# Moving the split of constant tables, the low parts of weights and the softmax scaling between engines in layer 0's mixer

## The chip, the cores and the metric

The kernel runs on one core of a Trainium2 chip. The metric is the device time of one execution in microseconds (us); the time of a version is the median of several executions. The core's engines are TensorE (PE; its weight loads are shown as PEld), VectorE (DVE), ScalarE (ACT), GpSimd (POOL) and SyncE (SP). Each works through a queue of its own in a fixed order, and waits on semaphores where it needs another's result. In this kernel SP issues all data transfers (DMAs).

## The reference

One step of a two-layer backbone on 128 context and 512 latent tokens, width 1024, in float32. Each layer is half an FFN, a token mixer and half an FFN. Layer 0's mixer, which the change touches, is windowed attention and a Hyena long convolution side by side; layer 1's is a gated DeltaNet. Cut to the mixer of layer 0:

```python
def sink_softmax(logits, sink):
    s = jnp.broadcast_to(sink.astype(jnp.float32).reshape(1, KVH_A, G_A, 1, 1), logits.shape[:-1] + (1,))
    return jax.nn.softmax(jnp.concatenate([s, logits], axis=-1), axis=-1)[..., 1:]
...
def hyena_mixer(u3, conv_w, conv_b, w1, b1, f1, w2, b2, f2, w3, bias):
    length = u3.shape[1]
    u3 = depthwise_conv(u3, conv_w) + conv_b
    x1, x2, v = jnp.split(u3, 3, axis=-1)
    kf = jnp.fft.rfft(hyena_filter(length, w1, b1, f1, w2, b2, f2, w3), n=2 * length, axis=0)
    z = v.astype(jnp.float32)
    for o, gate in enumerate((x1, x2)):
        y = jnp.fft.irfft(jnp.fft.rfft(z, n=2 * length, axis=1) * kf[None, :, o], n=2 * length, axis=1)[:, :length]
        z = gate.astype(jnp.float32) * (y + z * bias[o].astype(jnp.float32))
    return z.astype(u3.dtype)

def attn_hyena_mixer(h, ctx_kv, w_in, w_out, q_norm, k_norm, sink, conv_w, conv_b,
                     w1, b1, f1, w2, b2, f2, w3, hy_bias):
    ...
    y = hyena_mixer(u3, conv_w, conv_b, w1, b1, f1, w2, b2, f2, w3, hy_bias)
    return jnp.concatenate([a, y], axis=-1) @ w_out, k, v
```

## The kernel before

Matrices are multiplied in two parts: a value is split into a high part (rounded to the matmul's type, `fp32r`) and a low part, the float32 rest. For a weight tile that has come in by DMA, ACT makes the high part (line 453) and another engine subtracts it from the raw tile for the low part (line 458; `lo_eng`, DVE in this stage). For the Hyena part's constant Fourier tables `c_fwd` (forward) and `c_inv` (inverse), `load_split` (line 871) does the same in chunks of up to 1024 columns: the load (879), the high part by a cast on DVE (880), the low part by a subtraction on DVE (881). Loaded chunks lie in arena buffers (`base`, `HX`) that are freed after their split and used again; the split tables lie in `H`.

Layer 0's mixer (`mixer0`) runs its work in two stages. In the first, `merge` interleaves four generators: the projections u3 of the Hyena input (`u3_proj`: matmuls at line 487, then a short convolution at 1118 to 1120 and a store to `u_scratch` at 1336), attention (`attn`), the Hyena filters (`filters`: lines 948 to 1089 among others) and parts of the modulation, "ada" (529, 533, 587). In attention a group is four heads of one 128-token block. Its scores (1256 to 1263) are masked and their maximum is taken by DVE (1268), ACT takes exponentials (1274), DVE the reciprocal of the sum (1280); DVE then scales each of the four tiles (1282), PE transposes it (1126), and the copies of the transposed tiles (1289, 1291) go into the product with v (1301). There are ten groups, so 40 scalings.

In the second stage `beside` interleaves `hyena` with more ada work. `hyena` loads z from `u_scratch` (1351), splits both tables (1354, 1355), and for each order and half makes even and odd parts of z (DVE, 1392 to 1395) in buffers `eo[0]` and `eo[1]`, which have the names `base` and `HX` in the rows. PE transposes these (1397, 1398), ACT and DVE split the transposed parts (865, 868), and the forward transform follows (914), then the products with the filters' spectrum (1375 to 1380, DVE and POOL) and the inverse transform (1439).

The order on each engine is made by a scheduler: an instruction carries the value that `tc.cur_priority` had when it was written (a lower value comes sooner), and among those that can run by its own estimates the lowest goes first. So the written order, this priority and the buffers' reuse decide the queues together. SP's queue is in order too.

Of the kernel before, what the change touches and what calls it, by code (L numbers as in the profile page):

```python
# [326 lines left out]
class Step:  # L327
# [540 lines left out]
        self.nc.vector.tensor_tensor(out=out_lo, in0=src, in1=out_hi_f, op=ALU.subtract)  # L868


    def load_split(self, name, n, R):

        nc, A = self.nc, self.A
        t = R.alloc(2 * n)
        done = 0
        while done < n:
            m = min(1024, n - done)
            r = A.alloc(m)
            nc.sync.dma_start(out=r.f, in_=self.io[name][:, done:done + m])
            nc.vector.tensor_copy(out=t.r()[:, done:done + m], in_=r.f)  # L880
            nc.vector.tensor_tensor(out=t.r()[:, n + done:n + done + m], in0=r.f, in1=t.f[:, done:done + m], op=ALU.subtract)
            r.free()
            done += m
        return t
# [347 lines left out]
    def attn(self, oc, rg):  # L1232
# [7 lines left out]
        for blk in range(NTILE):  # L1240
# [5 lines left out]
            for kv in range(2):  # L1246
# [32 lines left out]
                nc.vector.tensor_tensor(out=z[:, 4, :], in0=z[:, 3, :], in1=z[:, 2, :], op=ALU.add)  # L1279
                nc.vector.reciprocal(out=z[:, 5, :], in_=z[:, 4, :])  # L1280
                for t in range(4):
                    nc.vector.tensor_scalar(out=pbs[t], in0=pbs[t], scalar1=z[:, 5, t:t + 1], scalar2=None, op0=ALU.mult)
                    p = rg.bank()
                    s.transposes(p, [pbs[t][:, 128 * c:128 * c + 128] for c in range(nch)])
                    cp = nc.scalar.activation if t % 2 else None
                    dst = pt[:, 0:nch, t, :]
                    src = p[:, :128 * nch].rearrange("p (c q) -> p c q", q=128)
                    if cp:
                        nc.scalar.activation(out=dst, in_=src, func=AF.Copy)
                    else:  # L1290
                        nc.vector.tensor_copy(out=dst, in_=src)
                    yield 110.0 * nch
# [47 lines left out]
    def hyena(self, oc, rg):  # L1340
# [10 lines left out]
                nc.sync.dma_start(out=t[half][c].f, in_=s.u_sc[6 * half + 2 * ((k + 2) % 3) + c])  # L1351

        load(zs, 0, 0)
        fw = s.load_split("c_fwd", s.FW, RH)
        iv = s.load_split("c_inv", GW, RH)
        ihi, ilo = iv.r()[:, :GW], iv.r()[:, GW:]
        prm = A.alloc(768)
        nc.sync.dma_start(out=prm.f, in_=s.io["c_prm"])
# [127 lines left out]
    def mixer0(self, done, beside_attn, beside_hyena):  # L1486
        A, s = self.A, self
        s.x_save(0)
        s.hx(F32)
        s.spare(F32)  # L1490
        oc = A.alloc(4 * NT)
        s.attn_alloc()
        nc = self.nc
        nc.vector.tensor_scalar(out=s.att_small.f[:, 2:10], in0=s.att_small.f[:, 2:10], scalar1=-1.0, scalar2=None, op0=ALU.mult)
        yield from s.attn_in()
        s.norm_save(0)
        s.filters_load(A)
        yield from s.filters_open(s.ring(2, 3), A)
        rf = s.ring(*[(3, 128 * i, 128) for i in range(4)])
        s.wides, s.by_half = [0], True  # L1500
        yield from merge((s.u3_proj(), 78.0), (s.attn(oc, s.rg), 78.0),
                         (s.filters(s.ring((2, 0, 256), (2, 256, 256)), rf, A), 100.0),
                         (beside_attn(rf), 20.0))
        s.wides, s.by_half = [0, 2], False
        s.attn_free()
        oh = A.arenas[0].alloc(4 * NT)
        side = beside_hyena()
        yield next(side)
        yield from beside(s.hyena(oh, s.ring(0, 1, 2, 3, 4, 5)), 100.0, side, 40.0)
        yield from side  # L1510
        ob, mh, ml = s.split_oc([b.f[:, NT * t:NT * t + NT] for b in (oc, oh) for t in range(4)])
        oc.free()
        oh.free()
        s.norm_load(0)
        s.x_load(0)
        s.h_next(False)
        yield from s.out_proj(1, mh, ml, 0, lambda t, xt: done(t, xt, s.tn.f, s.sq.f))
        for b in ob + [s.tn, s.sq]:
            b.free()
# [661 lines left out]
```

## Time and profile before

| | us |
|---|---|
| median of 3 executions | 3015.36 |
| the three | 3014.49, 3015.36, 3030.77 |
| the profiled execution | 3024.78 |
| its span | 3023.0 |
| PE busy in the span | 2887.1 (96%) |
| DVE / ACT / POOL busy | 2058.8 / 1642.4 / 1094.3 (68 / 54 / 36%) |

The first stage of layer 0's mixer lies at about 590 to 858 us of the span, the Hyena stage from there to about 1015 us. The busy shares are those of the whole span; what an engine does within a stage is read from windows, its waits and a timeline, and the rows for this stand below. A row of the timeline gives the start, the length, the engine, the line of the kernel, the operation, output and inputs with their shapes, and in brackets how long the engine had stood idle and for what.

### The profile page before, as it was taken

What the parts mean: (1) busy time and instruction counts of PE and PEld (TensorE: products, weight loads), DVE (VectorE), ACT (ScalarE), POOL (GpSimd) and SP (SyncE); (2) the same over time, 40 slices, a digit from 0 to 9 for tenths busy, and PEclk for the clock granted to TensorE, in tenths of its full rate; (3) what the DMA queues carried; (4) which work ended last, traced back from release to release, by engine and by line L of the source; (5) the groups of instructions that cost most, each with busy time, mean ns of one, the idle gap of its engine ahead of it and who ended that gap; (6) DMA issues with size and microseconds to landing.
All of it is one profiled execution on the core that took longest, in us unless ns stands there. A gap on an engine that the chain in (4) does not pass through costs nothing. (4 is left out here: it accounts for less than half of the span.)

```text
span 3023.0 us, 54115 instructions
## 1 busy us (share of the span) xinstructions
PE 2887.1 (96%) x20612; PEld 2686.1 (89%) x20612; DVE 2058.8 (68%) x4771; ACT 1642.4 (54%) x3325; POOL 1094.3 (36%) x958
## 2 busy tenths in 40 slices
PE   5999999999979999999999999999998999999999
PEld 3999999977856899999899999978888889999999
DVE  6747476587865675747674747577889977756473
ACT  5737374365622373838383747445555544748382
POOL 3525253101223462525552535322222224625260
PEclk7999999999989999999999999998999999999999
DMA  5434343334276222222122222331221012122222
GB/s 206 147 105 157 102 154 125 129 99 124 89 259 224 89 70 81 82 83 85 63 76 82 84 82 89 129 92 54 84 60 37 31 38 96 64 83 83 79 84 77
DMA packets 109440, 300.82 MB, mean 100 GB/s; under 512 B 11803, under 2 KB 31963, under 8 KB 104444
## 3 DMA queue, kind: packets, MB, share of 16 engines
q1 hardware_dynamic: 109180, 297.36, 29.8%
q8 instruction: 162, 2.65, 0.4%
q14 instruction: 98, 0.80, 0.1%
HBM read 277.39 MB, written 19.93 MB: 98 GB/s over the span
## 5 line engine op out<-in xcount | busy, mean ns | idle before, releaser
L453 ACT ACTIVATE wh<-base 128x512 fp32r<-128x512 f32 (+2 forms) x779 | 546.0, 706 | 600.5 <-PE psum L487 390.3
L487 PE MATMUL psum<-G,wh 128*128 128x320 f32 x4992 | 742.6, 310 | 9.2 <-DVE base L743 8.7
L487 PEld LDWEIGHTS psum<-G,wh 128*128 128x128 f32 x4992 | 736.5, 188 | 15.2 <-ACT wh L453 9.4
L448 POOL TENSOR_TENSOR base<-base 128x512 f32<-128x512 f32 x352 | 494.3, 1409 | 660.8 <-DVE wh L458 365.1
L787 PE MATMUL psum<-H,wh 128*128 128x322 f32 x4224 | 694.6, 316 | 17.0 <-ACT base L792 8.6
L787 PEld LDWEIGHTS psum<-H,wh 128*128 128x128 f32 x4224 | 648.4, 192 | 28.7 <-ACT base L792 10.6
L787 PE MATMUL psum<-HX,wh 128*128 128x322 f32 x3168 | 521.1, 313 | 0.0
L787 PEld LDWEIGHTS psum<-HX,wh 128*128 128x128 f32 x3168 | 482.8, 190 | 4.8 <-issue 4.2
L458 DVE TENSOR_TENSOR wh<-base,psum 128x512 fp32r<-128x512 f32 x559 | 381.4, 684 | 152.7 <-ACT psum L456 119.1
L487 PE MATMUL psum<-H,wh 128*128 128x322 f32 (+1 forms) x2448 | 480.0, 332 | 3.4 <-DVE base L728 2.1
L487 PEld LDWEIGHTS psum<-H,wh 128*128 128x128 f32 x2448 | 377.7, 194 | 26.2 <-issue 18.3
L456 ACT ACTIVATE psum<-wh 128x512 f32<-128x512 f32 x559 | 334.6, 600 | 45.9 <-DVE base L743 26.1
L458 DVE TENSOR_TENSOR wh<-base,wh 128x896 fp32r<-128x896 f32 (+2 forms) x187 | 202.1, 1085 | 91.2 <-PE psum L487 37.2
L743 DVE SCALAR_TENSOR_TENSOR base<-psum,base 128x128 f32<-128x128 f32 x224 | 113.0, 547 | 218.0 <-PE psum L487 218.0
L763 DVE SCALAR_TENSOR_TENSOR base<-base 128x128 f32<-128x128 f32 (+1 forms) x176 | 96.1, 552 | 123.1 <-POOL base L812 122.9
L458 POOL TENSOR_TENSOR wh<-base,wh 128x1024 fp32r<-128x1024 f32 x33 | 82.7, 2507 | 240.8 <-ACT wh L453 236.1
L801 POOL TENSOR_TENSOR base<-base 128x320 f32<-128x320 f32 x88 | 82.0, 932 | 161.4 <-DVE base L800 99.6
L809 ACT ACTIVATE base<-base 128x128 f32<-128x128 f32 (+2 forms) x264 | 114.8, 469 | 35.2 <-DVE base L804 17.4
L700 POOL TENSOR_TENSOR base<-base 128x640 f32<-128x640 f32 x30 | 76.3, 2544 | 112.1 <-ACT base L698 109.2
L766 ACT ACTIVATE G<-base 128x640 fp32r<-128x640 f32 x88 | 65.1, 740 | 90.3 <-DVE base L763 90.0
L767 DVE TENSOR_TENSOR G<-base,G 128x640 fp32r<-128x640 f32 x88 | 85.3, 969 | 21.5 <-ACT G L766 21.2
L812 POOL TENSOR_TENSOR base<-base 128x320 f32<-128x320 f32 x88 | 77.8, 884 | 44.0 <-DVE base L811 39.0
(700 smaller groups left out, 3746.6 us busy)
## 6 DMA issues: line engine op xcount, KB each, us to landing
base<-w SPq DMA_DIRECT2D x208, 512.0 KB, 3.2
base<-ada_w SPq DMA_DIRECT2D x128, 256.0 KB, 3.9
base<-w SPq DMA_DIRECT2D x64, 448.0 KB, 3.3
base<-dn_in SPq DMA_DIRECT2D x33, 512.0 KB, 3.3
base<-ada_w SPq DMA_DIRECT2D x14, 1024.0 KB, 5.0
G<-ada_w SPq DMA_DIRECT2D x48, 256.0 KB, 3.5
HX<-ada_w SPq DMA_DIRECT2D x10, 1024.0 KB, 4.9
base<-mx_in SPq DMA_DIRECT2D x18, 512.0 KB, 3.3
```

What stands on the lines that cost most here:

```text
L448: nc.gpsimd.tensor_tensor(out=out, in0=x, in1=y, op=op)
L453: nc.scalar.activation(out=hi, in_=src, func=AF.Copy)
L456: nc.scalar.activation(out=cp, in_=hif, func=AF.Copy)
L458: (self.lo_eng if q is None else nc.vector).tensor_tensor(out=lo, in0=src, in1=hif, op=ALU.subtract)
L487: nc.tensor.matmul(ps[:, HALF * h:HALF * h + n], lhsT=w[:, k, :], rhs=m[k][:, HALF * h:HALF * h + n], start=start and k == 0 and w is hi a ...
L743: nc.vector.scalar_tensor_tensor(out=xt[:, v], in0=ps[:, v], scalar=gate[:, t, c:c + 1], in1=xt[:, v], op0=ALU.mult, op1=ALU.add)
L763: nc.vector.scalar_tensor_tensor(out=tg[:, v], in0=tu[:, v], scalar=tu[:, HALF + k:HALF + k + 1], in1=tg[:, v], op0=ALU.add, op1=ALU.mult)
L767: TT(out=halves(gl[m]), in0=v, in1=halves(gf[m]), op=ALU.subtract)
L787: nc.tensor.matmul(dst[:, :HB], lhsT=w[:, i, :], rhs=v[:, i, :], start=not more and i == 0 and n == 0, stop=i == 3 and n == 2, skip_group_ ...
L801: nc.gpsimd.tensor_tensor(out=p5, in0=u2[:, 0, :HALF], in1=p5, op=ALU.add)
L809: nc.scalar.activation(out=tg[:, v], in_=tg[:, v], func=AF.Silu, bias=tg[:, HALF + k:HALF + k + 1])
L812: nc.gpsimd.tensor_tensor(out=u2[:, 0, :HALF], in0=u2[:, 0, :HALF], in1=fac[:, 0, :HALF], op=ALU.mult)
```

## The change

`load_split` lets ACT make the high part of each chunk, and takes the engine for the low part as an argument: DVE for `c_fwd`, GpSimd for `c_inv`. Both calls are given a priority value 100 higher, so later. Attention's scaling (1282) goes to GpSimd. While the first stage is written, `lo_eng` is GpSimd, so the low parts of the weights loaded there are made by it, except for tiles whose form is excluded at line 458. Lines behind 1355 move by 2, behind 1500 by 3 or 4: the old 1392 to 1398 are 1394 to 1400 in the new kernel.

```diff
-    def load_split(self, name, n, R):
+    def load_split(self, name, n, R, eng):
...
-            nc.vector.tensor_copy(out=t.r()[:, done:done + m], in_=r.f)
-            nc.vector.tensor_tensor(out=t.r()[:, n + done:n + done + m], in0=r.f, in1=t.f[:, done:done + m], op=ALU.subtract)
+            nc.scalar.activation(out=t.r()[:, done:done + m], in_=r.f, func=AF.Copy)
+            eng.tensor_tensor(out=t.r()[:, n + done:n + done + m], in0=r.f, in1=t.f[:, done:done + m], op=ALU.subtract)
...
-                    nc.vector.tensor_scalar(out=pbs[t], in0=pbs[t], scalar1=z[:, 5, t:t + 1], scalar2=None, op0=ALU.mult)
+                    nc.gpsimd.tensor_scalar(out=pbs[t], in0=pbs[t], scalar1=z[:, 5, t:t + 1], scalar2=None, op0=ALU.mult)
...
-        fw = s.load_split("c_fwd", s.FW, RH)
-        iv = s.load_split("c_inv", GW, RH)
+        self.tc.cur_priority += 100
+        fw = s.load_split("c_fwd", s.FW, RH, nc.vector)
+        iv = s.load_split("c_inv", GW, RH, nc.gpsimd)
+        self.tc.cur_priority -= 100
...
+        s.lo_eng = nc.gpsimd
         yield from merge((s.u3_proj(), 78.0), (s.attn(oc, s.rg), 78.0),
                          (s.filters(s.ring((2, 0, 256), (2, 256, 256)), rf, A), 100.0),
                          (beside_attn(rf), 20.0))
         s.wides, s.by_half = [0, 2], False
+        s.lo_eng = nc.vector
```

What it does to the queues is seen at the passage from the first stage to the Hyena stage. The rows give line, operation, output and inputs, and in brackets the semaphores that are waited for (DMAHW: a transfer's landing).

DVE before, from the copy that waits for u's load to the even and odd parts of the first half:

```order
L1395 COPY base<-base 128x1 [waits DMAHW5_49]
L880 CAST H<-HX 128x1024 [waits DMAHW6_49]
L881 TENSOR_TENSOR H<-HX,H 128x1024 [waits DVE_49]
L880 CAST H<-HX 128x1024 [waits DMAHW7_49]
L881 TENSOR_TENSOR H<-HX,H 128x1024 [waits DVE_49]
L880 CAST H<-HX 128x1024 [waits DMAHW0_49]
L880 CAST H<-base 128x266 [waits DMAHW1_49]
L881 TENSOR_TENSOR H<-HX,H 128x1024 [waits DVE_49]
L881 TENSOR_TENSOR H<-base,H 128x266 [waits DVE_49]
L1392 TENSOR_TENSOR base<-base 128x255 [waits DVE_49]
L1393 TENSOR_TENSOR base<-base 128x255
L1394 COPY base<-base 128x1
```

And DVE after, from the subtraction of a `c_fwd` chunk on:

```order
L881 TENSOR_TENSOR H<-HX,H 128x1024 [waits DMAHW3_49,Activation_49]
L1397 COPY base<-base 128x1 [waits DMAHW5_49]
L556 TENSOR_REDUCE base<-psum 128x8 [waits PE_49,Activation_49]
L557 TENSOR_TENSOR base<-base 128x8 [waits DVE_49]
L881 TENSOR_TENSOR H<-HX,H 128x1024 [waits DMAHW0_49,Activation_49]
L1394 TENSOR_TENSOR base<-base 128x255 [waits DMAHW3_49,Pool_49]
L1395 TENSOR_TENSOR base<-base 128x255
L1396 COPY base<-base 128x1
L1394 TENSOR_TENSOR base<-base 128x255 [waits DMAHW4_49,PE_49]
```

The casts and `c_inv`'s subtractions are gone from DVE, and the first operation on the even part of `base` has a wait on POOL now. POOL after, in the same place (before, it had nothing between line 1088 and the products of line 1377):

```order
L1088 MEMSET G_5048 1x128 [waits Pool_49]
L458 TENSOR_TENSOR wh<-base,wh 128x1024 [waits DMAHW6_49,PE_49,Activation_49]
L881 TENSOR_TENSOR H<-HX,H 128x1024 [waits DMAHW1_49,PE_49,Activation_49]
L881 TENSOR_TENSOR H<-HX,H 128x1024 [waits DMAHW2_49,Activation_49]
L881 TENSOR_TENSOR H<-base,H 128x266 [waits DMAHW5_49,DMAHW3_49,Activation_49]
L1379 TENSOR_TENSOR HX<-HX 128x256 [waits DMAHW7_49,DVE_49,Pool_49]
```

POOL has a weight's low part and the three subtractions of `c_inv` in a row there, each behind ACT's cast and the chunk's landing. PE before, from the transposes of ada's rows to the forward transform:

```order
L1126 MATMUL psum<-base 128x128 [waits Activation_49]
L1126 MATMUL psum<-base 128x128 x3
L1397 MATMUL psum<-base 128x128 [waits DMAHW1_49,DVE_49]
L1398 MATMUL psum<-base 128x128 [waits DVE_49]
L1397 MATMUL psum<-base 128x128 [waits DVE_49]
...
L1398 MATMUL psum<-base,HX 128x128
L529 MATMUL psum<-base 32x512 [waits DMAHW3_49]
L914 MATMUL psum<-G_7734,H 128x256 [waits Activation_49]
```

And after:

```order
L1126 MATMUL psum<-base 128x128 [waits Activation_49]
L1126 MATMUL psum<-base 128x128 x3
L529 MATMUL psum<-base 32x512 [waits DMAHW6_49]
L529 MATMUL psum<-base 32x512 x3
L1399 MATMUL psum<-base 128x128 [waits DMAHW3_49,DVE_49]
L1400 MATMUL psum<-base 128x128 [waits DVE_49]
L1399 MATMUL psum<-base 128x128 [waits DVE_49]
...
L1400 MATMUL psum<-base,HX 128x128
L914 MATMUL psum<-G_7734,H 128x256 [waits Activation_49]
```

The four ada matmuls of line 529 stand ahead of the eight transposes, where they stood behind them.

## Rows read from the trace of the kernel before

**Rows 1.** The page's head: span and number of instructions.
```profile
span 3023.0 us, 54115 instructions
```

**Rows 2.** Windows: from:to, length, busy us of PE, PEld, DVE, ACT, POOL, clock, DMA.
```profile
590.00:858.00 268.00, 260.81 (x1788) 205.12 (x1787) 208.90 (x627) 156.13 (x336) 42.21 (x90) 0.99 0.38 118
...
860.00:870.00 10.00, 0.00 (x0) 0.00 (x0) 6.02 (x13) 0.00 (x0) 0.00 (x0) 0.50 0.92 291
```

**Rows 3.** PE's waits 590 to 858 us: line, waited for, us in all, times, longest.
```profile
PE psum L1058 <- DVE G L1034: 2.7, 1, 2.7
```

**Rows 4.** PE's waits 858 to 1100 us.
```profile
PE psum L1397 <- DVE base L1392: 14.6, 1, 14.6
```

**Rows 5.** Timeline 836 to 885 us: start, length, engine, line, operation, wait.
```profile
843.00 9.54 PE L487 MATMUL psum<-H,wh 128*128 128x322 f32 x63
...
857.66 0.88 DVE L1120 SCALAR_TENSOR_TENSOR HX<-HX,base 128x641 f32<-128x641 f32 x1
...
858.57 0.33 SPq L1336 DMA_DIRECT2D u_scratch<-HX  x1
...
859.47 0.41 SPq L879 DMA_DIRECT2D HX<-c_fwd  x1
...
861.74 0.81 SPq L879 DMA_DIRECT2D HX<-c_inv  x2
...
863.18 0.15 DVE L1395 COPY base<-base 128x1 f32<-128x1 f32 x1 [2.74 <-DMA base<-u_scratch]
864.47 0.69 DVE L880 CAST H<-HX 128x1024 fp32r<-128x1024 f32 x1 [1.14 <-DMA HX<-c_fwd]
...
869.01 1.22 DVE L881 TENSOR_TENSOR H<-HX,H 128x1024 fp32r<-128x1024 f32 x1
...
870.15 0.43 DVE L881 TENSOR_TENSOR H<-base,H 128x266 fp32r<-128x266 f32 x1
870.62 0.42 DVE L1392 TENSOR_TENSOR base<-base 128x255 f32<-128x255 f32 x1
...
871.10 0.47 PE L1397 MATMUL psum<-base 128*128 128x128 f32 x1 [14.56 <-DVE base L1392]
...
873.11 1.92 PE L529 MATMUL psum<-base 128*32 128x512 f32 x2
...
874.96 7.48 PE L914 MATMUL psum<-G,H 128*128 128x256 f32 x56
```

**Rows 6.** DVE's groups by form, 590 to 858 us: count, busy us, mean ns.
```profile
L458 DVE TENSOR_TENSOR wh<-base,wh 128x1024 fp32r<-128x1024 f32 x13 | 15.8, 1218 | 0.8 <-ACT wh L453 0.7
...
L1282 DVE TENSOR_SCALAR HX<-HX,base 128x512 f32<-128x512 f32 x13 | 6.2, 494 | 0.1
```

**Rows 7.** Forms of line 458 in the whole span, on POOL: min/median/max ns.
```profile
L458 POOL TENSOR_TENSOR wh<-base,wh x33: 2349/2402/3003, 1937.5 to 2496.5; 128x1024 fp32r<-128x1024 f32 x33
```

**Rows 8.** POOL's groups by form, 590 to 870 us.
```profile
L1087 POOL TENSOR_TENSOR G<-G 1x128 f32<-1x128 f32 x16 | 8.7, 543 | 14.3 <-DVE G L1072 9.4 <-DVE G L1084 4.0 <-DVE base L1279 0.9
L1086 POOL COPY G<-G 128x128 f32<-128x128 f32 x16 | 5.6, 353 | 1.0
...
L1159 POOL TENSOR_TENSOR base<-base 128x512 f32<-128x512 f32 x2 | 2.6, 1288 | 17.6 <-PE psum L1157 17.6
```

**Rows 9.** Line 1282's answer, its part on who waited for it.
```profile
  PEld psum L1126: 0.4, 2
```

**Rows 10.** Timeline 818 to 836 us.
```profile
823.93 0.55 DVE L1268 CUSTOM_DVE_ANT_0 G<-psum,base 128x384 f32<-128x384 f32 x1
...
829.80 1.21 DVE L458 TENSOR_TENSOR wh<-base,wh 128x1024 fp32r<-128x1024 f32 x1
...
830.02 1.30 POOL L1087 TENSOR_TENSOR G<-G 1x128 f32<-1x128 f32 x1 [1.57 <-DVE G L1072]
...
833.67 1.29 DVE L1282 TENSOR_SCALAR HX<-HX,base 128x384 f32<-128x384 f32 x3
```

**Rows 11.** ACT's groups by form, 590 to 858 us.
```profile
L453 ACT ACTIVATE wh<-base 128x1024 fp32r<-128x1024 f32 x13 | 13.7, 1053 | 18.9 <-PE psum L487 18.9
```

## The prediction

> **What bounds the kernel now.** I read the page's head first for the span [rows 1], then busy time by stretch for layer 0's mixer, where the change lies [rows 2]. From 590 to 858 us, where attention, the u3 projections, the filters and the ada work run interleaved, PE is busy 260.81 of 268.00 us, 97%, at a granted clock of 0.99. DVE, which the change unloads, is busy 208.90 us, ACT 156.13 us, POOL 42.21 us. So PE bounds that stage; all its idle time is 7.2 us, and the longest of its waits names another line than the edited ones, 2.7 us at L1058 for DVE's L1034 [rows 3]. That is the first thing to see: taking work off DVE there can win some 5 us at the most, however much is taken.
>
> The second thing is the passage to the Hyena part. From 860 to 870 us PE does nothing at all and DVE is busy 6.02 us [rows 2]; the waits of the next stretch have one row that dwarfs the rest, 14.6 us at L1397 for DVE's L1392 [rows 4]. The timeline shows why [rows 5]. The last u3 matmuls end at 843.00 + 9.54 = 852.54 us; DVE finishes u's last tile (L1120) at 858.54; SP then issues its store (858.57), the second c_fwd load (859.47) and the c_inv loads (861.74). DVE splits each arrived chunk in its queue (cast L880, 0.69 us; subtraction L881, 1.22 us; from 864.47 to 870.58), and L1392, which makes what PE transposes first, stands behind all of it at 870.62. PE starts at 871.10. The first transform matmuls (L914) start at 874.96.
>
> **The change part by part.** *Weights' low parts (L458) and softmax scaling (L1282) to GpSimd.* On DVE they are 13 subtractions of 128x1024 at 1.218 us, 15.8 us, and 40 scalings at about 0.42 us (13 of 128x512 took 6.2 us), some 17 us [rows 6]. Some 31 of DVE's 208.90 us go, since two of the subtractions stay on DVE by the order. Since PE has 7.2 us of idle time in the stage, this brings between 0 and 4 us. On POOL a 128x1024 subtraction of the same line takes 2.402 us at the median elsewhere in this program [rows 7]; twelve stand in POOL's new order, 29 us. A tensor_scalar on POOL isn't in the trace. Its nearest rows are a 128x512 tensor_tensor at 1.288 us and a 128x128 copy at 0.353 us [rows 8]: scaled to 512 elements that is at most 1.3 us by the one, and as little as 0.8 by the other (four copies less three times a fixed part of some 0.2 us, an estimate); L458's rate, 2.35 ns an element, gives 1.2. I take 1.0, so 40 tiles are some 35 us (bounds 25 to 50). POOL goes from 42 to about 106 of 268 us: far from a bound by itself. What counts is the delay of each group of four tiles, since PE's transposes of that group (L1126) wait for the scaled tiles. On DVE a group's four take 1.7 to 2.0 us, on POOL 3 to 5: 1.5 to 3 us later, and up to 2.4 us more where an L458 stands ahead in POOL's queue.
>
> Is there cover? In the whole stage PE's weight load for L1126 waited 0.4 us, twice, for the scaling [rows 9], so the order of before is matched to its chain with little to spare: in the last group the last score reduction (L1268) starts at 823.93, the scaling at 833.67, 9.7 us on [rows 10], and the transposes follow at once. By the order of after, PE has between a group's last score matmul and its first transpose some 8 us of other work in two of the ten groups and 10.5 to 18 us in the others (the matmuls that stand between, counted, at what each kind takes before: an L487 9.54 / 63 = 0.151 us [rows 5]; an estimate). A chain without a queue in front (reduction 0.55, exponentials, sums, reciprocal, as the pieces of the same stretch) needs some 6 to 7 us. So the two short groups lose perhaps 1 to 3 us each, the others nothing or little. With DVE's relief against it I take +2 us for the stage, bounds -3 and +9.
>
> *Table splits.* Six casts go from DVE to ACT, four of them of 0.69 us, and c_inv's three subtractions, two of 1.22 us and the 266-wide rest of 0.43 us, from DVE to POOL. ACT's casts cost what L453 of that shape does, 1.053 us [rows 11]; ACT has nothing else there. But the gate stays. In the order of after, DVE's addition on `base` (L1394, the old L1392) still stands ahead of PE's eight transposes and it has a wait on POOL there that it didn't have: it writes into the buffer that the raw c_inv rest lay in, so POOL's last subtraction has to be done. Nothing that DVE was relieved of is then on the path; the path is DMA, ACT, POOL. Counted from the end of the last u3 matmul: L1120 ends about 1 us sooner, at +5.0 instead of +6.0, since the cast L880 and L1392 no longer stand in front of it. SP issues c_fwd at about +5.5 and the second piece of c_inv, which waits for the landing of u's store, at +8.3 (861.74 is 3.17 us behind 858.57). It lands at +11.6 to +12.5 (before, the c_fwd chunk took 5.0 us from 859.47 to its cast at 864.47, with both loads beside it). ACT casts the pieces by about +13.4. POOL begins with the first c_inv piece at about +11.5 and needs 2.40 + 2.40 us and 0.7 us for the rest: +17.1. Then L1394 (0.42 us), and the transposes at +17.6 where they stood at 871.10 - 852.54 = +18.6. A gain of 1.0; from +16.4 (loads in 3 us) to +20 (POOL at 3.0 us, loads late) all is possible.
>
> *Order on PE.* The four ada matmuls that stood between the transposes and L914 (873.11, 1.92 us [rows 5]) come ahead of the transposes now, so they fall into the idle time. L914 then follows ACT's and DVE's split of the transposed parts alone, about 2.7 us behind the first transpose instead of 3.86: another 1.2 us. *Sum for the passage:* -1.0 - 1.2 = -2.2, bounds -4.5 and +1.5. The matmuls behind it, and everything outside the mixer, keep their order; for the side work in the Hyena part that slides I give 1.5 us either way.
>
> **One rule against the change.** At 829.80 DVE's L458, which reads two SBUF operands, runs for 1.21 us; POOL's L1087, begun at 830.02, took 1.30 us, 0.76 over its mean of 0.543 [rows 8, 10]. The Trainium skill, page "SBUF — State Buffer", section "Who interferes with whom", says that a VectorE instruction with two SBUF inputs contends with a GpSimd instruction that reads SBUF, and that the one issued second waits for the first to finish. This row agrees with it. On that rule each moved instruction can lose as much as a neighbour on DVE lasts, and DVE as much as POOL's. It is the third rival below, with a price from the rows.
>
> **The rivals.** *The idle time goes.* If POOL and ACT were done before u is, the transposes would be bound by u's own return: its load (issued after the store) let DVE's L1395 go at 863.18 [rows 5], and c_fwd's low part, which L914 needs, can't be ready before some 866.7 (864.47 + 1.05 + 1.22). Then L914 starts near 867, 8 us sooner: 3007. For it: DVE's queue is what ends the wait now. Against it: the order shows the same buffer behind it and POOL's subtractions are twice as long.
>
> *Slower: POOL holds up the softmax.* Each group gets 1.5 to 3 us more for the scaling, 2.4 us where an L458 is ahead, and the filters' POOL steps (L1074), which PE's next filter matmuls wait for, queue behind both. It decides from the point where the sum passes what a group has to spare, some 2 us in the short groups and 4 in the others. With 3 us of stall in each of eight groups that is +24, less the passage's 2.2: 3037; with the filters' waits, another us for each group, 3045; with 2 us in all a group, 3029. For it: the cover was used up in the last group of before. Against it: PE's order was made anew with the scaling in POOL's queue, and DVE's queue ahead of the chain is shorter.
>
> *Collisions on the operands.* If the 0.76 us of [rows 8, 10] hit every one of a group's four tiles, that is 3 us a group on top, of which the groups with 10 us and more absorb most: +4 to +5 in the two short ones together, +2 to +4 in the rest and +1 in the passage. Added to +2 and -2.2 that is about +8: 3023.
>
> **How the numbers follow.** The profiled execution took 3024.78 us, of which the span [rows 1] is nearly all; the median of three is 3015.36, and the parts are differences, so I take them from the median: -2.2 + 2 = -0.2, and 3015.2. The parts' bounds, added in quadrature rather than end to end, are about -6 and +8: 3009 to 3023. Chances: this forecast 0.70; the idle time goes, 0.08; collisions, 0.10; POOL holds up the softmax, 0.12. The bound of 0.5%, about what a measurement of this kernel tells from no change, is 15 us. Faster by more would take nearly all of PE's idle time at both places (14.6 and 7.2 us): 0.03. Slower by more (over 3030.4): most of the softmax case, and a little of the collisions: 0.11. Same: 0.86. The range takes in the first rival and the collisions: 3006 to 3025.
>
> **What would show it.** Right: PE stays at about 97% from 590 to 858 us; DVE there falls by some 30 us to 175 and POOL rises to about 105; the wait at the first L1399 names L1394 still, 12 to 14 us long, with POOL's last L881 ending just before it; L1126 has 2 to 5 us of waits on POOL in all. Wrong: the wait at L1399 under 8 us (the gate was elsewhere), waits on POOL's L1282, L458 or L1074 of over 10 us (POOL costs more than its nearest rows), or POOL's L1282 outside 0.5 to 1.3 us.

## The result, and the profile after

The changed kernel took 3054.64 us (median of 4, 3051.74 to 3064.7) where the one before took 3014.93 in the same comparison: a ratio of 1.0126, 95% interval 1.0108 to 1.0144. Measured again, beside the kernels that have two of its parts, it gave 1.0122 (1.0103 to 1.0140). It is slower by some 38 us. The forecast of 3015.2 us, no change, was wrong, and the range of 3006 to 3025 didn't hold the time.

The profiled execution took 3051.74 us, its span 3050.0. PE waits now for the scaling where it waited 0.4 us [rows 9]. The rows are PE's waits from 590 to 885 us (waited for, us in all, times, longest):

```profile
PE psum L1126 <- POOL HX L1282: 13.7, 25, 1.1
PE psum L1126 <- POOL G L1282: 3.3, 5, 0.8
```

I read each run in three pieces: the first stage, from 590 us to the end of the last u3 matmul (L487); the passage, from there to the first transform matmul (L914); and the rest of the mixer, up to the first matmul of line 787 in the layer's second half-FFN. Windows of before over the first two pieces (from:to, length, busy us of PE, PEld, DVE, ACT, POOL, clock, DMA share, GB/s):

```profile
590.00:852.54 262.54, 258.31 (x1772) 204.38 (x1775) 204.30 (x618) 152.87 (x332) 42.21 (x90) 0.99 0.37 113
852.54:874.96 22.42, 6.37 (x31) 2.47 (x31) 15.34 (x30) 4.34 (x7) 0.00 (x0) 0.65 0.92 327
```

and of the changed kernel:

```profile
590.00:884.94 294.94, 269.70 (x1774) 205.92 (x1776) 196.52 (x567) 150.97 (x330) 114.21 (x141) 0.97 0.34 107
884.94:908.78 23.84, 6.99 (x37) 2.79 (x37) 9.86 (x24) 8.81 (x13) 5.28 (x3) 0.59 0.91 319
```

So the first stage went from 262.5 to 294.9 us, 32.4 more: PE's idle time in it from 4.2 to 25.2 us, of which the two rows on L1126 are 17.0, and its busy time up by 11.4. The passage went from 22.4 to 23.8 us. The first L787 matmul went from 1055.05 to 1091.54 us, 36.5 later, so the rest of the mixer adds 2.7. That mark is what the experiments are compared by beside the measured ratio, since what lies behind it, the same number of matmuls in all kernels, varied by up to 18.7 us over the profiled executions.

The fixed start of 590 us has a weakness: it isn't the same point of the program in each execution. Attention's first score matmul (L1256), which has the same 4178 matmuls ahead of it in every kernel, starts between 589.43 and 592.82 us. A run that comes to it early shows a stage that is too short by as much. So the table below also has the stage counted from that matmul, as the difference from the 259.9 us of before (592.61 to 852.53); where a reading hangs on a few microseconds, that column decides. Two executions of the changed kernel still differ by 3 us in it.

The price of the moved work on POOL (groups by form, 590 to 880 us; count, busy us, mean ns, idle time ahead):

```profile
L458 POOL TENSOR_TENSOR wh<-base,wh 128x1024 fp32r<-128x1024 f32 x11 | 26.4, 2397 | 22.5 <-ACT wh L453 21.3 <-ACT G L1028 1.1
L1282 POOL TENSOR_SCALAR HX<-HX,base 128x512 f32<-128x512 f32 x13 | 20.2, 1562 | 9.6 <-DVE base L1280 7.7 <-PE psum L487 1.9
...
L1282 POOL TENSOR_SCALAR HX<-HX,base 128x384 f32<-128x384 f32 x12 | 14.9, 1248 | 3.0 <-DVE base L1280 3.0
...
L1282 POOL TENSOR_SCALAR HX<-HX,base 128x128 f32<-128x128 f32 x7 | 4.1, 608 | 9.7 <-ACT G L1011 9.7
```

A weight's low part costs 2.397 us, as in [rows 7]. A scaling costs 1.562 us for 512 elements, 1.248 for 384 and 0.608 for 128: 2.48 ns an element and 0.29 fixed; all 40 take 49.6 us. How PE meets that is seen in one group, the second of 384 columns (timeline 674 to 681 us):

```profile
674.92 0.18 DVE L1280 RECIPROCAL base<-base 128x4 f32<-128x4 f32 x1
...
675.27 2.46 POOL L1282 TENSOR_SCALAR HX<-HX,base 128x384 f32<-128x384 f32 x2 [0.77 <-DVE base L1280]
...
676.57 0.55 PE L1126 MATMUL psum<-base,HX 128*128 128x128 f32 x3 [0.66 <-POOL HX L1282]
...
677.71 1.24 POOL L1282 TENSOR_SCALAR G<-G,base 128x384 f32<-128x384 f32 x1
...
677.79 0.55 PE L1126 MATMUL psum<-base,HX 128*128 128x128 f32 x3 [0.67 <-POOL HX L1282]
...
678.93 1.24 POOL L1282 TENSOR_SCALAR HX<-HX,base 128x384 f32<-128x384 f32 x1
...
679.01 0.55 PE L1126 MATMUL psum<-base,G 128*128 128x128 f32 x3 [0.67 <-POOL G L1282]
...
680.23 0.55 PE L1126 MATMUL psum<-base,HX 128*128 128x128 f32 x3 [0.68 <-POOL HX L1282]
```

DVE's reciprocal (L1280) is done, POOL scales the four tiles one after the other, and PE's three transposes of each tile follow at once and wait 0.66 to 0.68 us for the next. Four tiles cost 2.7 us of idle time in this group. It is not one wait that work ahead of the first transpose could cover, but one for each tile, since in this group PE's order has nothing between the four tiles.

The passage (timeline 855 to 912 us) answers to [rows 5]:

```profile
867.27 17.66 PE L487 MATMUL psum<-H,wh 128*128 128x322 f32 x118
...
889.91 0.89 DVE L1120 SCALAR_TENSOR_TENSOR HX<-HX,base 128x641 f32<-128x641 f32 x1
...
890.83 0.33 SPq L1336 DMA_DIRECT2D u_scratch<-HX  x1
891.25 0.38 SPq L879 DMA_DIRECT2D HX<-c_fwd  x1
891.96 5.08 SPq L879 DMA_DIRECT2D HX<-c_inv  x2
...
895.80 1.94 PE L529 MATMUL psum<-base 128*32 128x512 f32 x8 [4.32 <-DMA base<-ada_w]
...
897.88 1.06 ACT L880 ACTIVATE H<-HX 128x1024 fp32r<-128x1024 f32 x1 [7.57 <-DMA HX<-c_fwd]
...
900.30 4.80 POOL L881 TENSOR_TENSOR H<-HX,H 128x1024 fp32r<-128x1024 f32 x2 [26.03 <-ACT H L880]
...
905.05 0.65 POOL L881 TENSOR_TENSOR H<-base,H 128x266 fp32r<-128x266 f32 x1
905.74 0.42 DVE L1394 TENSOR_TENSOR base<-base 128x255 f32<-128x255 f32 x1 [5.54 <-POOL H L881]
...
906.22 0.47 PE L1399 MATMUL psum<-base 128*128 128x128 f32 x1 [8.48 <-DVE base L1394]
...
908.78 3.63 PE L914 MATMUL psum<-G,H 128*128 128x256 f32 x15 [0.47 <-ACT G L865]
```

From the end of the last u3 matmul (867.27 + 17.66 = 884.93) the rows read: L1120 done at +5.9, c_fwd issued at +6.3, cast by ACT at +13.0; c_inv's second issue held up in SP's queue (891.96 and 5.08 us long, two loads); POOL's two subtractions from +15.4 to +20.2, its third to +20.8; L1394 at +20.8; transposes at +21.3; L914 at +23.8.

### The profile page after: what moved, and what is told of

Same layout as the page of the kernel before. It is cut to its first block, busy times and chain, and to the rows that moved or that the text cites. A ratio compares the mean times of both kernels' runs of the same rounds, so it can differ in the third digit from the quotient of the medians.

```text
span 3050.0 us, 54175 instructions
## 1 busy us (share of the span) xinstructions
PE 2893.3 (95%) x20612; PEld 2682.4 (88%) x20612; DVE 2046.8 (67%) x4710; ACT 1644.1 (54%) x3329; POOL 1174.1 (38%) x1013
## 3 DMA queue, kind: packets, MB, share of 16 engines
q8 instruction: 162, 2.65, 0.4%
## 5 line engine op out<-in xcount | busy, mean ns | idle before, releaser
L487 PE MATMUL psum<-G,wh 128*128 128x320 f32 x4992 | 742.9, 310 | 9.2 <-DVE base L743 8.7
L487 PEld LDWEIGHTS psum<-G,wh 128*128 128x128 f32 x4992 | 736.9, 188 | 15.1 <-ACT wh L453 9.4
L787 PE MATMUL psum<-H,wh 128*128 128x322 f32 x4224 | 697.5, 317 | 15.0 <-ACT base L792 8.0
L787 PEld LDWEIGHTS psum<-H,wh 128*128 128x128 f32 x4224 | 651.0, 193 | 27.0 <-ACT base L792 10.2
L787 PE MATMUL psum<-HX,wh 128*128 128x322 f32 x3168 | 520.9, 313 | 0.0
L787 PEld LDWEIGHTS psum<-HX,wh 128*128 128x128 f32 x3168 | 482.6, 190 | 4.8 <-issue 4.2
L458 DVE TENSOR_TENSOR wh<-base,psum 128x512 fp32r<-128x512 f32 x559 | 381.2, 684 | 152.8 <-ACT psum L456 119.3
L487 PE MATMUL psum<-H,wh 128*128 128x322 f32 (+1 forms) x2448 | 470.1, 328 | 2.8 <-DVE base L728 1.5
L487 PEld LDWEIGHTS psum<-H,wh 128*128 128x128 f32 x2448 | 372.2, 191 | 23.5 <-issue 16.3
L458 DVE TENSOR_TENSOR wh<-base,wh 128x896 fp32r<-128x896 f32 (+2 forms) x175 | 187.4, 1075 | 91.9 <-PE psum L487 36.8
L458 POOL TENSOR_TENSOR wh<-base,wh 128x1024 fp32r<-128x1024 f32 x45 | 111.6, 2480 | 263.1 <-ACT wh L453 257.2
L809 ACT ACTIVATE base<-base 128x128 f32<-128x128 f32 (+2 forms) x264 | 114.4, 467 | 34.2 <-DVE base L804 18.2
L767 DVE TENSOR_TENSOR G<-base,G 128x640 fp32r<-128x640 f32 x88 | 85.3, 970 | 21.2 <-ACT G L766 20.8
```

What stands on the lines that cost most here:

```text
L458: (self.lo_eng if q is None else nc.vector).tensor_tensor(out=lo, in0=src, in1=hif, op=ALU.subtract)
L487: nc.tensor.matmul(ps[:, HALF * h:HALF * h + n], lhsT=w[:, k, :], rhs=m[k][:, HALF * h:HALF * h + n], start=start and k == 0 and w is hi a ...
L767: TT(out=halves(gl[m]), in0=v, in1=halves(gf[m]), op=ALU.subtract)
L787: nc.tensor.matmul(dst[:, :HB], lhsT=w[:, i, :], rhs=v[:, i, :], start=not more and i == 0 and n == 0, stop=i == 3 and n == 2, skip_group_ ...
L809: nc.scalar.activation(out=tg[:, v], in_=tg[:, v], func=AF.Silu, bias=tg[:, HALF + k:HALF + k + 1])
```

## The experiments

One table for all runs. The ratio is against the kernel before on the same chip, with its 95% interval. Stage and passage are in us, as defined above; "from L1256" is the change of the stage when it is counted from that matmul, and the last column is the shift of the first L787 matmul against 1055.05. These four are from the one profiled execution of each run. Differences in the medians are against the kernel before beside the same runs, which took 3019 to 3023 us there; the first expectations name absolute times, worked out from its 3015.

| run | ratio (95%) | stage | from L1256 | passage | L787 |
|---|---|---|---|---|---|
| before | | 262.5 | | 22.4 | |
| changed | 1.0126 (1.0108, 1.0144) | 294.9 | +32.2 | 23.8 | +36.5 |
| changed, again | 1.0122 (1.0103, 1.0140) | 297.6 | +35.4 | 23.4 | +38.7 |
| scaling back on DVE | 0.9998 (0.9982, 1.0014) | 266.9 | +7.4 | 14.2 | -1.5 |
| scaling alone | 1.0044 (1.0028, 1.0060) | 289.1 | +27.3 | 13.4 | +17.6 |
| low parts alone | 1.0001 (0.9983, 1.0019) | 268.1 | +7.2 | 19.7 | +2.0 |
| tables alone | 0.9992 (0.9972, 1.0012) | 260.1 | -0.2 | 22.6 | -1.9 |
| scaling, low parts | 1.0100 (1.0079, 1.0122) | 295.9 | +34.2 | 13.9 | +26.7 |
| scaling, tables | 1.0075 (1.0055, 1.0095) | 286.8 | +27.4 | 11.2 | +21.0 |
| before, buffers first | 0.9978 (0.9962, 0.9993) | 262.1 | +1.5 | 13.7 | -4.4 |
| changed, buffers first | 1.0090 (1.0069, 1.0110) | 298.8 | +36.3 | 9.9 | +31.2 |
| tables, buffers first | 0.9988 (0.9973, 1.0002) | 261.8 | +0.1 | 12.1 | -4.3 |
| half the scaling | 0.9995 (0.9979, 1.0011) | 268.8 | +7.3 | 13.2 | -0.6 |
| scaling on ACT | 0.9978 (0.9963, 0.9992) | 264.2 | +3.3 | 12.9 | -7.7 |
| scaling on ACT, buffers first | 1.0022 (1.0009, 1.0034) | 261.1 | +1.2 | 14.1 | -1.6 |
| changed, scaling on ACT | 1.0029 (1.0014, 1.0043) | 272.4 | +11.0 | 22.3 | +11.2 |

### Which part costs the time

The first theory was that the scaling carries the loss alone; its rivals were POOL's queue with the low parts, and the tables. The changed kernel with the scaling back:

```diff
-                    nc.gpsimd.tensor_scalar(out=pbs[t], in0=pbs[t], scalar1=z[:, 5, t:t + 1], ...
+                    nc.vector.tensor_scalar(out=pbs[t], in0=pbs[t], scalar1=z[:, 5, t:t + 1], ...
```

> The changed kernel with only the softmax scaling (L1282) back on DVE; weights' low parts on GpSimd and the new table splits stay. Scaling theory (each tile's transposes wait for GpSimd's 1.25 to 1.56 us scaling): 3012 to 3022, and no wait at L1126 of note. Queue-and-collision theory (GpSimd's 2.4 us low parts and their collisions with DVE carry the loss): still over 3035. Table theory (the new splits cost over 10 us at the passage): 3025 to 3035.

Measured: 0.9998, no change against before. Without the scaling on GpSimd the loss is gone. That isn't to say that the other parts are free: the stage is 7.4 us longer here, counted from L1256, and the passage 8.2 shorter, so a loss and a gain cancel.

The kernel before with the opposite edit, the scaling alone:

> The kernel before with only the softmax scaling moved to GpSimd. Scaling theory: 3038 to 3055, waits at L1126 on GpSimd's L1282 of 15 to 20 us in all, over 0.5 us for each of some 30 tiles. Queue-and-collision theory: under 3030, since nothing long stands in GpSimd's queue. Table theory: under 3030.

Measured: 1.0044, which is +13 us; +16 in the medians. PE's waits for L1282 from 590 to 880 us:

```profile
PE psum L1126 <- POOL HX L1282: 14.4, 24, 1.6
PE psum L1126 <- POOL G L1282: 4.9, 8, 0.9
```

That is 19.3 us, as the scaling theory had it, and the stage is 26.6 us longer (27.3 from L1256); but the whole is not the 38 us. The passage took 13.4 us in place of 22.4 and gave 9.0 back (rows of its timeline):

```profile
886.55 0.43 DVE L881 TENSOR_TENSOR H<-base,H 128x266 fp32r<-128x266 f32 x1
...
887.01 0.42 DVE L1392 TENSOR_TENSOR base<-base 128x255 f32<-128x255 f32 x1
...
887.49 0.48 PE L1397 MATMUL psum<-base 128*128 128x128 f32 x1 [4.38 <-DVE base L1392]
...
892.49 0.80 PE L914 MATMUL psum<-G,H 128*128 128x256 f32 x2
```

Here DVE splits the 266-wide rest of c_inv at 886.55, ahead of the two large pieces, and L1392 follows it at 887.01. In [rows 5] the rest came last.

The kernel before with `s.lo_eng = nc.gpsimd` around the first stage:

> The kernel before with only the weights' low parts (L458) of the first stage on GpSimd. Scaling theory: 3010 to 3018, PE busy 97% from 590 to 853 us as before. Queue-and-collision theory: 3025 to 3040, with waits of PE's L487 for L458 or of L1078 behind L1074. Table theory: as the scaling theory.

Measured: 1.0001. The stage is 5.5 us longer (7.2 from L1256), which the scaling theory didn't have, and the passage 2.7 shorter. PE has 4.9 us of waits at L592 and L948 for DVE's L1072. The timeline shows the longest of them (699 to 702.2 us):

```profile
699.14 2.34 POOL L458 TENSOR_TENSOR wh<-base,wh 128x1024 fp32r<-128x1024 f32 x1
...
699.56 2.20 DVE L1041 TENSOR_TENSOR G<-G 128x256 f32<-128x256 f32 x1
...
701.68 0.28 DVE L1072 TENSOR_TENSOR G<-psum,G 128x128 f32<-128x128 f32 x1
...
702.01 0.33 PE L592 MATMUL psum<-base 128*128 128x128 f32 x1 [1.93 <-DVE G L1072]
```

L1041 took 0.428 us in the mean of before's stage. In this run nine instructions of DVE took 0.7 to 2.2 us more than the median of their form before, 14.3 us in all. Each ran beside an L458 on POOL, and each of the six waits for L1072 comes with such an instruction shortly ahead of L1072 in DVE's queue. In the run with the scaling alone no instruction of DVE was longer by more than 0.5 us. So it is the weights' subtractions on POOL that DVE runs into, and through DVE PE.

The kernel before with the new `load_split` and the priority alone:

> The kernel before with only the new table splits: casts on ACT, c_inv's low parts on GpSimd, priority 100 later. Scaling theory: 3012 to 3019; first transposes 17 to 21 us behind the last u3 matmul (18.6 before, 21.3 in the changed kernel). Queue-and-collision theory: 3010 to 3015, since GpSimd is free in this stage. Table theory: over 3025.

Measured: 0.9992, with the stage 0.2 us shorter from L1256 and the passage as it was, 22.6. The first transposes come 18.8 us behind the last u3 matmul.

### How the parts add up

Alone, the three cost +16, +3 and 0 us in the medians; together 38. Two runs with two parts each, and the changed kernel on the same chip:

> The changed kernel itself, beside the others on one chip. Additive theory (scaling alone costs +16 us, the other two parts nothing each, so together +16): +12 to +20 us against before. Interaction theory (the scaling costs some 26 us in the attention stage wherever it is made by GpSimd; alone it gets some 9 us back at the passage, where the buffer of the even part is free early; the changed kernel doesn't get that back): +30 to +42 us.

> Softmax scaling and weights' low parts on GpSimd, old table splits. DVE splits the c_inv rest early here and L1392 on the even part follows it at once. Additive theory: +16 us. Interaction by the passage: +14 to +22 us, first transposes 8 to 12 us behind the last u3 matmul. Interaction by GpSimd's queue (L458 in front of the scaling): +28 to +40 us, with waits at L1126 of over 25 us in all.

> Softmax scaling on GpSimd and the new table splits, weights' low parts on DVE. L1394 waits for GpSimd's split of the c_inv rest. Additive theory: +16 us. Interaction by the passage: +24 to +36 us, first transposes 16 to 21 us behind the last u3 matmul. Interaction by GpSimd's queue: +14 to +20 us.

Measured: 1.0122, 1.0100 and 1.0075. The additive theory falls. The time of scaling with low parts, 32 us in the medians, lies in the queue theory's range, but for another reason. With the low parts added to the scaling the stage grows from 289.1 to 295.9 us, and the passage stays short (13.9). That run's waits at L1126 for POOL are 16.9 us in all, under the 25 that the queue theory wanted, so the 6.8 us of the low parts come elsewhere in the stage. Here too nine instructions of DVE beside an L458 are longer than before, by 14.5 us in all. Scaling and tables together have the passage short as well, 11.2 us, which the passage theory had wrong for this run. Its timeline says why:

```profile
884.12 0.65 POOL L881 TENSOR_TENSOR H<-base,H 128x266 fp32r<-128x266 f32 x1 [17.61 <-ACT H L880]
884.81 0.42 DVE L1394 TENSOR_TENSOR base<-base 128x255 f32<-128x255 f32 x1 [0.78 <-POOL H L881]
...
885.29 0.48 PE L1399 MATMUL psum<-base 128*128 128x128 f32 x1 [4.26 <-DVE base L1394]
...
892.92 4.72 POOL L881 TENSOR_TENSOR H<-HX,H 128x1024 fp32r<-128x1024 f32 x2 [8.15 <-ACT H L880]
```

L1394 waits for POOL here too, but POOL takes the rest of c_inv first, at 884.12, and the two large pieces from 892.92 on. In the changed kernel they stand in front of it [the rows of the passage above], 4.8 us of POOL, each behind its load. So it is not the engine that splits c_inv, but the place of this one chunk in the order, that decides the passage; and the order is the scheduler's, made anew with each edit. All runs whose buffers stay where they were agree. With the rest's subtraction ahead of c_fwd's last piece and of both large pieces of c_inv, the passage takes 11.2 to 14.2 us; behind c_fwd's last piece (low parts alone) it takes 19.7; behind one large piece of c_inv too (tables alone), or both, 22.3 to 23.8.

From these the changed kernel's 36.5 us at L787 add up as: scaling in the first stage +26.6, low parts beside it +6.8, tables -1.0 (295.9 to 294.9), passage +1.4, rest of the mixer +2.7. The terms are good to some 3 us, by which the stage of the changed kernel itself differed between its two executions. What the other two combinations with the scaling won at the passage, 9 and 11 us, is what the changed kernel lacks.

### The buffer at the passage

If the chunk's buffer is what L1392 waits for, it has to go when the buffers of the even and odd parts are allocated ahead of the tables:

```diff
+        eo = [A.alloc(512) for _ in range(2)]
         load(zs, 0, 0)
...
-        eo = [A.alloc(512) for _ in range(2)]
```

> The kernel before with one line moved: the buffers of the even and odd parts are allocated ahead of the tables, so that no table chunk lies in them and L1392 waits for u alone. Buffer theory (the reuse of a chunk's buffer sets the 14.6 us at the passage): the wait falls to 5 to 9 us, 3 to 8 us less time than before. Queue theory (DVE's in-order splits set it, whatever the buffers): same as before.

Measured: 0.9978, 5.9 us faster in the medians; the wait at L1397 is 7.0 us in place of 14.6 [rows 4], the passage 13.7. The rest of the mixer gives 4.8 of the 8.7 us back.

> The changed kernel with the buffers of the even and odd parts allocated ahead of the tables, so that L1394 has no wait on GpSimd. Buffer theory: from the last u3 matmul to the first transpose 9 to 12 us in place of 21, 7 to 10 us less than the changed kernel: +27 to +31 us against before. Chain theory (ACT's casts, GpSimd's subtractions and the loads set the passage, whatever the buffers, since L914 needs the tables): still +35 to +40 us.

Measured: 1.0090, +28.5 us in the medians, as the buffer theory had it, with the first transposes 7.3 us behind the last u3 matmul and the passage 9.9 us. It is 7.5 us better at L787 than the changed kernel on the same chip, though the passage alone won 13.5: further on, PE stood waiting in the forward transform (PE's waits, 590 to 1060 us):

```profile
PE psum L914 <- DVE HX L1380: 5.5, 1, 5.5
```

The late tables are now in the way there: ahead of L1380, DVE waited for POOL's last subtraction of c_inv (timeline 914 to 918 us):

```profile
917.02 0.43 DVE L1378 TENSOR_TENSOR HX<-psum,G 128x256 f32<-128x256 f32 x1 [4.22 <-POOL H L881]
```

The same shows in the next run, which has the tables' part alone, with the buffers first:

> The kernel before with the new table splits and with the buffers of the even and odd parts allocated ahead of the tables; scaling and weights' low parts stay on DVE. Buffer theory: the wait at L1399 falls from 14.5 us (tables alone) to 4 to 8 us, and the kernel is 6 to 12 us faster than before. Chain theory: no change beyond 3 us.

Measured: 0.9988, its interval reaching 1. The passage is 10.3 us shorter, as wanted, but the rest of the mixer 6.8 longer; the kernel is not 6 to 12 us faster.

### What it is about the scaling

Is it the price of a tile on GpSimd, or that a group has to pass through another queue? Every second tile of the kernel before to GpSimd:

```diff
+                    (nc.gpsimd if t % 2 else nc.vector).tensor_scalar(out=pbs[t], in0=pbs[t], ...
```

> The kernel before with only every second of a group's four scalings on GpSimd. Price theory (GpSimd's 1.25 to 1.56 us a tile, one after the other, is what the transposes wait for): the first stage (590 us to the last u3 matmul) is 8 to 16 us longer than the 262.5 of before, in place of 26.6 with all four. Handoff theory (a group that has to pass through GpSimd's queue at all loses its 2.6 us): 22 to 28 us longer.

Measured: the stage is 6.3 us longer, less than a half of 26.6 and under what either theory wanted (7.3 against 27.3 from L1256); each group passes through POOL here too, so the handoff alone isn't it. PE's waits at L1126 from 590 to 880 us:

```profile
PE psum L1126 <- POOL HX L1282: 4.4, 7, 1.7
...
PE psum L1126 <- POOL G L1282: 1.3, 2, 0.8
```

5.7 us in place of 19.3: two tiles that are ready early let POOL run beside them. And all four on ACT:

```diff
+                    nc.scalar.activation(out=pbs[t], in_=pbs[t], func=AF.Copy, scale=z[:, 5, t:t + 1])
```

> The kernel before with the softmax scaling on ACT, which copies with a scale. Price theory (a tile takes 0.4 to 0.8 us there): the first stage is 2 to 10 us longer than before. Handoff theory (any engine but DVE, which made the reciprocal, costs the group): over 18 us longer.

Measured: 0.9978 (3.5 us in the medians). The stage is 3.3 us longer from L1256, a tile takes what these groups say (ACT, 590 to 860 us):

```profile
L1282 ACT ACTIVATE HX<-HX,base 128x512 f32<-128x512 f32 x13 | 8.6, 713 | 0.9 <-DVE base L733 0.9
...
L1282 ACT ACTIVATE HX<-HX,base 128x384 f32<-128x384 f32 x12 | 6.8, 608 | 1.2 <-DVE base L1280 1.1
```

0.713 and 0.608 us where POOL took 1.562 and 1.248; PE didn't wait at L1126 for it. The order came out with the c_inv rest early, so the passage is 12.9 us, and that, not the scaling, makes the kernel faster than before. With the changed kernel's other parts it is otherwise:

> The changed kernel with the softmax scaling on ACT in place of GpSimd; weights' low parts and c_inv's low parts stay on GpSimd. Scaling theory (the loss hangs on GpSimd's price for the scaling): within 6 us of before, first stage 264 to 270 us. Queue theory (the low parts on GpSimd and the wait of L1394 on GpSimd cost about 15 us by themselves when the scaling is off DVE): 12 to 22 us slower than before.

Measured: 1.0029, between the two theories. The stage is 272.4 us, 8.2 more than with the scaling on ACT alone, and the passage 22.3. So the low parts on GpSimd cost 7 to 8 us of the first stage in each company, counted from L1256: 7.2 alone, 34.2 against 27.3 beside the scaling, 11.0 against 3.3 beside the scaling on ACT, and 7.4 with the scaling back on DVE (in the last two the tables, which alone took nothing, are in as well), and the order at the passage is the slow one again.

Both edits that won, together:

> The kernel before with the softmax scaling on ACT and the buffers of the even and odd parts allocated ahead of the tables. Shared theory (both edits save the same idle time at the passage): as either alone, 5 to 9 us faster than before, passage 11 to 14 us from the last u3 matmul to L914. Additive theory: 11 to 15 us faster.

Measured: 1.0022, slower than before and than either alone, which neither theory has. The passage, 14.1 us, is the shared gain; the rest of the mixer is 8.1 us longer than that of before in the profile. 4.3 of them are one wait in the forward transform, for the instruction that is L1380 in the changed kernel, with a late chunk of c_inv ahead of it in DVE's queue (timeline 868 to 902 us):

```profile
878.50 0.69 DVE L880 CAST H<-HX 128x1024 fp32r<-128x1024 f32 x1 [2.10 <-DMA HX<-c_inv]
879.23 1.23 DVE L881 TENSOR_TENSOR H<-HX,H 128x1024 fp32r<-128x1024 f32 x1
...
880.90 0.42 DVE L1378 TENSOR_TENSOR HX<-psum,G 128x256 f32<-128x256 f32 x1
...
881.38 1.65 PE L914 MATMUL psum<-G,H 128*128 128x256 f32 x6 [4.33 <-DVE HX L1378]
```

So the time won at the passage is lost again where the tables are needed. Another 3.5 us are PE's busy time (175.1 against 171.6, at a granted clock of 0.96 against 0.98), whose cause I leave open. So two versions beat the kernel before, by 0.22% each in the ratio: the scaling on ACT, and the buffers first.

## Why the prediction was wrong, point by point

**PE bounds the first stage, and DVE's relief is worth little.** Right; up to the last u3 matmul PE's idle time was even less than the 7.2 us I read, 4.2, since the window to 858 takes in some of the passage. DVE lost 30.6 us of work there, the sum of the moved instructions' times, and its busy time, in which overlapping instructions count once, fell by only 7.8, from 204.30 to 196.52: operations that stayed took longer, 15 us in the sum of their groups. Eight instructions beside an L458 on POOL make up most of it (14.4 us over the medians of before). One group of before and then of after (count, busy us, mean ns):

```profile
L1043 DVE TENSOR_TENSOR HX<-G 128x128 f32<-128x128 f32 x32 | 9.5, 312 | 0.0
```

```profile
L1043 DVE TENSOR_TENSOR HX<-G 128x128 f32<-128x128 f32 x32 | 11.9, 385 | 0.1
```

**A scaling on POOL costs 1.0 us, 0.8 to 1.3, at 512 elements.** This is the first step that failed. It took 1.562 us, and 40 of them 49.6 us against the 35 I took and the 50 I allowed. The nearest row I leaned on was the copy; a two-operand subtraction at 2.35 ns an element [rows 7] with a fixed part was the right one (2.48 ns and 0.29 us).

**Only the two short groups lose.** This is the step that failed most. I set the work between a group's last score matmul and its first transpose against one delay for the group. But POOL starts when DVE's reciprocal is done, and from then on each tile can be a wait of its own: 1.24 us of POOL against 0.55 us of its transposes at 384 elements, 1.56 against 0.66 at 512, four times, with nothing or a few short matmuls of PE's order between them. The 40 tiles made 30 waits. The stage's term was +2 us, with bounds of -3 and +9; the whole stage measured +32.4, scaling alone +26.6. Only half of the tiles on POOL measured +6.3, so it is the price times four in a row that decides, as the rival "POOL holds up the softmax" had it: its price, 3 us for each of eight groups, 3037, or 3045 with the filters' waits, was near the 3054 that came. That is luck in part: the waits for the scaling were 17.0 us over all ten groups, not 24, and the rest of the stage's loss came as busy time and at other lines. I gave it 0.12, arguing that PE's order was made anew with the scaling in POOL's queue. But a new order doesn't spread what comes in a row: in the order of after the four tiles' transposes stand together in some groups, and in the others at most 16 short matmuls stand between two of them. Whether the scheduler's own estimate of POOL's scaling was too low, no run here shows.

**The low parts on POOL are free.** They cost 7 to 8 us of the stage, counted from L1256. I had counted their 2.4 us only where they stand in front of a scaling. What they do is hold up DVE: in the run with them alone 4.9 us of PE's waits, at L592 and L948, are for an L1072 that stood on DVE behind an instruction stretched beside an L458. The other 2 to 3 us aren't assigned.

**The gate at the passage stays, and the passage gains 2.2 us.** The mechanism held: L1394 waited for POOL's last subtraction (905.05 + 0.65, then 905.74). The size was off by 3.6: +1.4. L1120 was done at +5.9, not +5.0, since DVE stood 1.07 us for a landing at L1394 on `HX`, which is in front of it now; the second c_inv load was issued 5.9 us behind u's store (the row at 891.96 ends at 897.04, and one issue takes 0.3 to 0.4) where I took 3.17 from before; the loads themselves took 6.6 us (c_fwd, 891.25 to 897.88) against 5.0. PE's four ada matmuls moved into the idle time as foreseen; the first of them waited 4.3 us for its load, at no cost; behind them the wait at the first L1399 is 8.5 us in place of the 12 to 14 that I named as the sign.

**The idle time goes.** Its size is what the runs with a short passage show: 10 to 14 us from the last u3 matmul to L914, 8 to 12 less than before. Its mechanism, u's return as the next bound, is seen in two of them, before and tables with the buffers first, where the first L1392 (L1394) waited 3.7 and 2.7 us for the load from `u_scratch`; in the others it came behind a table's cast or subtraction. I had ruled it out for this order, rightly; that it hung on which chunk lay in the buffer, and so on the order, I hadn't seen.

**Collisions on the operands.** They are real, but not where I priced them: the scalings on POOL stretch nothing on DVE by more than 0.5 us in the run with the scaling alone, and the weights' subtractions stretch eight or nine instructions of DVE in each of the five runs with them that I went through, by 14.3 to 15.3 us in all. In the changed kernel with the scaling on DVE, one scaling ran into a low part on POOL (timeline 722 to 730 us):

```profile
721.85 0.48 DVE L1282 TENSOR_SCALAR HX<-HX,base 128x512 f32<-128x512 f32 x1
...
725.31 2.65 DVE L1282 TENSOR_SCALAR HX<-HX,base 128x512 f32<-128x512 f32 x1
725.32 2.35 POOL L458 TENSOR_TENSOR wh<-base,wh 128x1024 fp32r<-128x1024 f32 x1 [5.17 <-ACT wh L453]
```

2.65 us in place of 0.48 while POOL's L458 ran for 2.35. The Trainium skill, "SBUF — State Buffer", "Who interferes with whom", says of `tensor_scalar` on VectorE that it can enter the modes that contend with GpSimd; this row agrees with it. By my price this rival gave +8 in the end, and the low parts' 7 to 8 us are of that size; but they are not the loss, which goes with the scaling: the run with the scaling back on DVE, collisions and all, was 0.9998, its shorter passage against its longer stage.

## What to carry to other kernels

When work on the path of the bounding engine moves to another engine, compare the price of one item there with the time the bounding engine needs for the item before: if it is longer, each item of the chain can be a wait, and slack ahead of the first covers the first alone. Price an operation that the trace doesn't show by the dearest near row per element, and give the loss that follows from it the larger chance. Look also at what the moved work does to the engine that it left: here its neighbours there grew by half of what had gone. And where a step waits for a buffer, ask which chunk lies in it and where that chunk stands in the order: moving one line of allocation won as much as any change of engine here.

## What the runs showed that I hadn't expected

A `tensor_scalar` of one tensor with a column of scalars costs GpSimd 2.48 ns an element and 0.29 us, about as much as a subtraction of two tensors (2.35 ns an element in all), and more than the 128x512 multiplication of L1159 (1.29 us against 1.56). On ACT the same scaling takes 0.713 us for 512 elements. A subtraction of 2.4 us on GpSimd can hold an instruction of VectorE that runs beside it until it ends, whatever that one's own length: 2.20 us for an L1041 of 0.43. A transpose group that stands alone is dearer than in a row by the profile, in which the ends of matmuls are modelled: the 120 transposes of L1126 took 26.2 us of PE's busy time in the changed kernel's stage where they took 19.5 before, part of the 11.4 us by which PE's busy time rose. The rest of that rise I can't assign; the granted clock of the stage's windows was 0.97 against 0.99.
